# A fourth seven-product pair in every pass over w_down, in a float32 transformer block on one core

## The chip, the cores and the metric

The kernel runs on one core of a Trainium2 chip. The metric is the device time of one execution in microseconds (us), as a median of several executions. Engines are named as in the profile: PE multiplies matrices (its weight loads are PEld), DVE and ACT are the vector and the scalar engine, POOL and SP issue DMA transfers here (POOL the ones that convert or accumulate, SP the plain ones).

## What is computed

One layer over 256 tokens of width 2048, all in float32. The first half (attention and convolution) is not touched by the change. The second half is a gated feed-forward network with 5632 hidden columns:

```python
hn = rms_norm(h, norm2_g[l])
a = jnp.einsum('bsd,df->bsf', hn, w_gate[l])
bu = jnp.einsum('bsd,df->bsf', hn, w_up[l])
h = h + jnp.einsum('bsf,fd->bsd', jax.nn.silu(a) * bu, w_down[l])
```

## The kernel before

**Products.** A float32 factor is split into a rounded part (hi) and the remainder (lo). A product of two factors takes three matmuls: hi by hi, lo by hi, hi by lo. Each matmul has 128 rows, a 128x128 stationary block and 512 moving columns.

**Blocks.** The hidden columns come in 11 blocks of 512 (j0 to j10). For each block w_gate and w_up are multiplied side by side, then u = silu(a) * bu is transposed and stored as factors for w_down. w_down is taken after the blocks j0 to j3, after j4 to j7 and after j8 to j10: here these are the groups A, B and C. A group is multiplied in two passes (n = 0 and n = 2) of two column blocks of 512 each, so there are six passes: A0, A2, B0, B2, C0, C2. Results are added to the output in memory by POOL's DMAs; the last pass reads its own column block back (`so_far`) and writes the sum.

**Units.** A pass is a string of units, written out by hand in `ORDER` and `DOWN`. Two neighbouring 128-row slices of w_down make a "two". A unit `g` or `u` multiplies one two with one of the pass's two column blocks: 12 matmuls. A unit `s` (a "pair") multiplies a two with both column blocks by seven products in place of eight (the scheme of Strassen and Winograd): 21 matmuls in place of 24. In an `s` the weight blocks are first combined on DVE (`pair_sums`), rounded on ACT (`round_raw` for the three raw blocks, `round_pair` for the four sums) and split on DVE (`split_pair`). The factors are combined too (`pair_forms`). For a `g` or `u` there is one rounding on ACT (L342) and one subtraction on DVE (L351). Where the letter is upper-case, ACT writes the negative and a DMA of POOL adds the weights to it (L345, L346), so that DVE has nothing to do.

**Buffers.** Raw weights of pairs have two buffers (`wb`), the sums one (`wt`), the rounded and the split weights of pairs two each (`wh`, `wl`). So a pair's raw rounding writes into the buffer that PE has to be done with two pairs earlier. The eight sums of products lie in eight PSUM banks, four called `acc` and four called `aux`. The aux banks are those of Q2, Q4, Q3 and QX, in the order in which a pass takes them; the bank of QX is taken only by the first `u`, and until then the transposed factors (`ps_a`) go through it. A new pass takes the old pass's banks: those of Q6, Q7, Q5, Q2 and Q4 come free as `bank_sums` (L1196 to L1201) reads them, and Q3's with the first of the two last additions (L1215 in `block_done`, L1249 in `down_done`). Q3 is the last of a pair's seven products (`PRODUCTS`).

**Order.** All instructions are issued in an order that is worked out when the program is built, and each engine runs its own in that order. Before unit t is multiplied, `run_chunks` issues in this order: the splits of units up to t+3, the raw rounding of pairs up to t+5, the weight sums of pairs up to t+5, the rounding of DMA units up to t+5, the rounding of all units up to t+4, and loads up to t+9. While a unit is multiplied, `resume()` lets the waiting pieces of work go one step on: four steps in a pair, two in a `g` or `u`. After a block the piece `block_done` adds and multiplies, waits five steps (`TO_TRANSPOSE`), transposes the first two of the block, and so on. A two that is kept as it is (`transposed`, L957 and L959) is ready three steps after its transposes; a two that serves a pair is ready six steps after them (`pair_forms`: steps 0, 2, 4 and 6). The second two's transposes come two steps after the first is ready. If a unit of w_down is reached before its factors are ready, `multiply_two` or `multiply_pair` issues steps until they are (`while not c["ready"](c): resume()`).

In the last block (j10) the factors of a two that is kept as it is are first copied to a buffer `ac` (L955), which for the second two has the tag `sum2`, the one that `pair_forms` uses for its sums `fs`.

Of the kernel before, what the change touches and what calls it, by code (L numbers as in the profile page):

```python
# [13 lines left out]
F32 = mybir.dt.float32  # L14
F32R = mybir.dt.float32r
AF = mybir.ActivationFunctionType
ALU = mybir.AluOpType
AX = mybir.AxisListType

P = 128  # L20
D = 2048
S = 256
NM = S // P
# [8 lines left out]
KD = D // P  # L32
N = 512
# [52 lines left out]

Q1, Q6, Q7, Q5, Q2, Q4, Q3, QX = range(8)

PRODUCTS = ((Q6, 5, 1), (Q7, 6, 2), (Q5, 4, 3), (Q1, 0, 5), (Q2, 1, 6), (Q4, 2, 0), (Q3, 3, 4))

DOWN = (dict(pairs=((1, 0), (1, 1), (2, 0)), order=("sgGsgGgsuUuUu",) * 2),
        dict(pairs=((4, 0), (4, 1), (5, 0)), order=("sgGsgGgsuUuUu",) * 2),
        dict(pairs=((8, 0), (8, 1), (9, 0)), order=("sGsGgsUUu", "sGsGGsUUu")))

RAW_AHEAD = 5
LOAD_AHEAD, DMA_AHEAD, SUMS_AHEAD, HI_AHEAD, LO_AHEAD = 9, 5, 5, 4, 3


BLOCKS = 2 * KD + 1

TO_TRANSPOSE = 5

# [12 lines left out]
def tile_block(  # L115
# [4 lines left out]
    nc = tc.nc  # L120
    PSUM = bass.MemoryType.PSUM
    act, dve, pool, pe, sp = nc.scalar, nc.vector, nc.gpsimd, nc.tensor, nc.sync
# [17 lines left out]
    make_identity(nc, ident)  # L140
    arena = [const.tile([P, BLOCKS, P], F32R, tag=f"l{x}", name=f"l{x}") for x in ("hi", "lo")]
    neghalf = once.tile([P, 8], F32, tag="neghalf", name="neghalf")
# [26 lines left out]
    def col(key, k):  # L169
        return cols[:, AT[key] + k : AT[key] + k + 1]  # L170
# [80 lines left out]
    def start(gen):  # L251
        running.append(gen)
# [13 lines left out]
    def room(n, hold=0):  # L266
        while held[0] + n > AUX:
            yield
        held[0] += hold
# [574 lines left out]
    def out_done(n, ps):  # L844
        cs = slice(n * N, (n + 1) * N)
        for m in range(NM):
            dve.tensor_tensor(h[m][:, cs], h[m][:, cs], ps[m], ALU.add)
        for m in range(NM):
            pool.dma_start(out=out[m * P : (m + 1) * P, cs], in_=h[m][:, cs])
        if n == 2:  # L850
            held[0] -= NM
        yield
        for t in range(0, N // P, 2):
            k = n * (N // P) + t
            yield from room(1)
# [12 lines left out]
            for i in range(2):  # L868
                hT[k + i] = (hi[:, i, :], lo[:, i, :])
            yield  # L870
        for m in range(NM):
            square_sum(h[m][:, cs], ss2[m][:, n : n + 1])
        if n == D // N - 1:
            yield
            for m in range(NM):
                ss = small.tile([P, 1], F32, tag="ssh", name="ssh")
                dve.tensor_reduce(ss, ss2[m], AX.X, ALU.add)
                rsqrt_mean(rstd2[m], ss, D, EPS)
            yield
            yield  # L880
            prestack.close()
            ffn["pool"] = fp = ctx.enter_context(tc.tile_pool(name="ffn", bufs=1))
            spare_lhs.extend(fp.tile([P, 2, 2, S], F32R, tag=f"a{x}", name=f"a{x}") for x in ("hi", "lo"))
            start(make_forms())


    ffn = {}
# [39 lines left out]
    def place(g):  # L927

        pairs = DOWN[g]["pairs"]
        at = 7 * len(pairs)  # L930
        fhi, flo = (a[:, :at].rearrange("p (f q) c -> p f q c", f=7) for a in arena)
        twos = [(j, t) for j in range(sum(FGROUPS[:g]), sum(FGROUPS[: g + 1])) for t in range(2) if (j, t) not in pairs]
        free = [arena_two(i) for i in range(at, BLOCKS - 3, 4)]
        free += [tuple(a[:, i] for a in spare_lhs) for i in range(2)]
        assert len(free) >= len(twos)
        down[g] = dict(forms=(fhi, flo), pairs=pairs, twos=twos, at=dict(zip(twos, free)), ready=set())

    down = {}
    spare_lhs = []
# [117 lines left out]
    def pair_sums(c):  # L1057

        b = c["b"]
        c["t"] = t = ffn["pool"].tile([P, 4, N], F32, tag="wt", name="wt")  # L1060
        dve.tensor_tensor(t[:, 2:4], b[:, 1:3], b[:, 0:1].to_broadcast([P, 2, N]), ALU.subtract)  # L1061
        dve.tensor_tensor(t[:, 1], b[:, 1], t[:, 3], ALU.add)
        dve.tensor_tensor(t[:, 0], t[:, 1], b[:, 3], ALU.subtract)  # L1063

    def round_raw(c):
        if "hi" not in c:
            c["hi"] = ffn["pool"].tile([P, 7, N], F32R, tag="wh", name="wh", bufs=2)
            act.copy(c["hi"][:, 4:], c["b"][:, 1:])  # L1068

    def round_pair(c):  # L1070
        round_raw(c)
        act.copy(c["hi"][:, :4], c["t"])  # L1072

    def split_pair(c):
        c["lo"] = ffn["pool"].tile([P, 7, N], F32R, tag="wl", name="wl", bufs=2)
        dve.tensor_tensor(c["lo"][:, 4:], c["b"][:, 1:], c["hi"][:, 4:].bitcast(F32), ALU.subtract)  # L1076
        dve.tensor_tensor(c["lo"][:, :4], c["t"], c["hi"][:, :4].bitcast(F32), ALU.subtract)  # L1077

    def sum_bank(c, i):
        sums = c["sums"]  # L1080
# [5 lines left out]
    def multiply_pair(c):  # L1086
        while not c["ready"](c):
            resume()
        (fhi, flo), p = c["forms"](), c["p"]
        products = PRODUCTS[3:4] + PRODUCTS[:3] + PRODUCTS[4:] if c["done"] else PRODUCTS  # L1090
        for n, (q, f, w) in enumerate(products):
# [51 lines left out]
    def fast_block(order, side_u, side_g, pairs, twos, **kw):  # L1143
# [3 lines left out]
        for unit in order:  # L1147
# [26 lines left out]
    def down_block(g, n):  # L1174

        last = g == len(FGROUPS) - 1 and n == D // N - 2
        ks = lambda jt: (jt[0] * (N // P) + 2 * jt[1], jt[0] * (N // P) + 2 * jt[1] + 1)
        pairs = DOWN[g]["pairs"]
        twos = [(j, t) for j in range(sum(FGROUPS[:g]), sum(FGROUPS[: g + 1])) for t in range(2) if (j, t) not in pairs]
        units = fast_block(DOWN[g]["order"][n // 2], ("w_down", n * N), ("w_down", (n + 1) * N),  # L1180
                           [(q, ks(jt)) for q, jt in enumerate(pairs)], [(jt, ks(jt)) for jt in twos],
# [9 lines left out]
    def bank_sums(q):  # L1191

        fp = ffn["pool"]
        w1 = halfway.pop("w1")
        u2, u3, w4 = (fp.tile([P, N], F32, tag=f"sum{i}", name=f"sum{i}") for i in range(1, 4))
        dve.tensor_tensor(u2, q[Q6], w1, ALU.add)  # L1196
        dve.tensor_tensor(u3, q[Q7], u2, ALU.add)
        dve.tensor_tensor(w4, q[Q5], u3, ALU.add)
        dve.tensor_tensor(u2, q[Q5], u2, ALU.add)  # L1199
        dve.tensor_tensor(w1, q[Q2], w1, ALU.add)  # L1200
        dve.tensor_tensor(u3, q[Q4], u3, ALU.add)  # L1201
        halfway.update(g=(w1, u3), u=(u2, w4))
# [21 lines left out]
    def down_products(n, q, last):  # L1224
        so_far = None
        if last:
            so_far = ffn["pool"].tile([P, 4, N], F32, tag="wt", name="so_far")[:, :NM]
            pool.dma_start(out=so_far, in_=out[:, n * N : (n + 1) * N].rearrange("(m p) n -> p m n", p=P))
        bank_sums(q)
        for m in range(NM):  # L1230
            add_to_out(m, n + 1, halfway["g"][m])
        yield
        if last:
            for m in range(NM):
                dve.tensor_tensor(halfway["u"][m], halfway["u"][m], so_far[:, m], ALU.add)
        halfway["added"] = True
# [104 lines left out]
```

## Time and profile before

| | us |
|---|---|
| median of three runs | 1040.02 (1039.77 to 1040.20) |
| the profiled execution | 1041.07 |
| its span, first to last instruction | 1039.2 |
| PE busy in the span | 1030.1 |
| DVE busy | 862.3 |
| ACT busy | 685.6 |

The profiled execution is 1.05 us above the median of the runs, and 1.87 us of it lie outside the span. PE's busy time is not PE at its peak, since matmuls overlap: one of 512 columns shows 389 ns in the profile, and the next starts 227 ns after it.

The second half as PE runs it, from the start of each block's first product to the start of the next block's (us from the span's start):

| block | from | to | us | matmuls of 512 columns |
|---|---|---|---|---|
| A0 | 513.03 | 555.47 | 42.44 | 183 |
| A2 | 555.47 | 596.95 | 41.48 | 183 |
| B0 | 763.05 | 805.50 | 42.45 | 183 |
| B2 | 805.50 | 846.98 | 41.48 | 183 |
| j10 | 929.54 | 971.31 | 41.77 | 180 |
| C0 | 971.31 | 1004.12 | 32.81 | 135 |
| C2 | 1004.12 | 1034.72 | 30.60 | 135 |

Times of C2 end where a further matmul would have started. A0, B0, j10 and C0 contain transposes besides.

### The profile page before, as it was taken

The numbers are of one execution on the slowest core, as the hardware profiler recorded it, in microseconds if no ns is written. First come the engines' busy times: TensorE is split into PE (matmuls) and PEld (weight loads), VectorE is DVE, ScalarE is ACT, GpSimd is POOL, SyncE is SP. The second block draws the span as 40 slices with busy tenths as digits, with TensorE's granted clock in tenths as the row PEclk, the third lists the DMA queues.
The fourth block names the chain that finished last, engine by engine and source line by source line (L and its number), as shares of the span: only waits on it lengthen the run. The fifth ranks groups of instructions, "written<-read, shape, count | busy, mean of one in ns | idle before, by whom it ended". The sixth has DMA issues, their size and how long they took to land.

```text
span 1039.2 us, 13042 instructions
## 1 busy us (share of the span) xinstructions
PE 1030.1 (99%) x4641; PEld 850.3 (82%) x4641; DVE 862.3 (83%) x1086; ACT 685.6 (66%) x864; POOL 155.4 (15%) x198
## 2 busy tenths in 40 slices
PE   8999999999999999999999999999999999999998
PEld 6888888888888888788888888888888888888886
DVE  5599989898546699999978789999896697998983
ACT  5855568766856567777556567776765666767761
POOL 0040133411100101001002120010001121101021
PEclk9999999999999999999999999999999999999999
DMA  9867766676566669898889998987969999879896
GB/s 357 302 202 211 238 206 213 187 211 176 163 201 231 230 215 281 241 323 240 257 246 298 257 306 267 309 229 249 307 187 285 300 271 331 235 243 298 250 249 129
DMA packets 65777, 258.05 MB, mean 248 GB/s; under 512 B 7344, under 2 KB 8624, under 8 KB 58288
## 3 DMA queue, kind: packets, MB, share of 16 engines
q1 hardware_dynamic: 48656, 201.34, 53.5%
q0 software_dynamic: 16768, 55.58, 28.2%
q8 instruction: 36, 0.59, 0.2%
q10 hardware_dynamic: 288, 0.29, 0.1%
q14 instruction: 29, 0.24, 0.1%
HBM read 248.80 MB, written 8.39 MB: 247 GB/s over the span
## 4 chain that ended last, share of the span: by engine, by line
PE 95%; DVE 2%; ACT 1%; issue 1%; DMA 1%; POOL 0%; SPq 0%; DVEq 0%
PE q L1116 11%; PE q L1120 11%; PE q L1115 11%; PE acc L387 11%; PE acc L382 11%; PE acc L381 11%; PE q L1094 9%; PE q L1096 8%; PE q L1095 8%; PE ps_a L922 1%; DMA raw<-in_wts_dram 1%; PE ps_s L731 1%; PE ps_o L809 0%; DVE y L596 0%; PE ps_h L859 0%
## 5 line engine op out<-in xcount | busy, mean ns | idle before, releaser
L342 ACT CAST whi<-raw 128x1024 fp32r<-128x1024 f32 (+1 forms) x261 | 270.3, 1046 | 105.1 <-PE acc L382 42.0
L351 DVE TENSOR_TENSOR wlo<-raw,whi 128x1024 fp32r<-128x1024 f32 (+1 forms) x173 | 209.0, 1218 | 72.9 <-ACT whi L342 71.4
L381 PE MATMUL acc<-whi,lhi 128*128 128x512 f32 x416 | 164.7, 396 | 1.5 <-ACT lhi L243 1.4
L382 PE MATMUL acc<-whi,llo 128*128 128x512 f32 x416 | 162.8, 391 | 0.7 <-DVE llo L244 0.7
L1077 DVE TENSOR_TENSOR wl<-wt,wh 128x2048 fp32r<-128x2048 f32 x58 | 132.7, 2287 | 20.6 <-ACT wh L1072 20.6
L1068 ACT CAST wh<-wb 128x1536 fp32r<-128x1536 f32 x58 | 86.0, 1483 | 87.5 <-PE q L1095 49.1
L346 POOL DMA_DIRECT2D wlo<-in_wts_dram x74 | 65.0, 889 | 510.4 <-ACT wlo L345 483.6
L1115 PE MATMUL q<-whi,chi 128*128 128x512 f32 x320 | 124.7, 390 | 0.0
L1116 PE MATMUL q<-whi,clo 128*128 128x512 f32 x320 | 124.6, 389 | 0.0
L1072 ACT CAST wh<-wt 128x2048 fp32r<-128x2048 f32 x58 | 110.4, 1904 | 18.5 <-DVE wt L1063 18.4
L1094 PE MATMUL q<-wh,fhi 128*128 128x512 f32 x280 | 109.2, 390 | 0.4 <-DVE sum L1199 0.4
L1096 PE MATMUL q<-wl,fhi 128*128 128x512 f32 x280 | 109.0, 389 | 0.0
L1095 PE MATMUL q<-wh,flo 128*128 128x512 f32 x280 | 109.0, 389 | 0.0
L596 DVE SCALAR_TENSOR_TENSOR y<-upad,cw,y 128x256 f32<-128x256 f32 x240 | 100.8, 488 | 5.3 <-ACT y L589 5.3
L1076 DVE TENSOR_TENSOR wl<-wb,wh 128x1536 fp32r<-128x1536 f32 x58 | 101.6, 1752 | 2.3 <-ACT wh L1068 2.3
L387 PE MATMUL acc<-wlo,lhi 128*128 128x512 f32 x368 | 101.4, 397 | 0.2 <-DVE wlo L351 0.2
L381 PEld LDWEIGHTS acc<-whi,lhi 128*128 128x128 f32 x416 | 78.5, 189 | 18.5 <-ACT lhi L243 1.8
L382 PEld LDWEIGHTS acc<-whi,llo 128*128 128x128 f32 x416 | 78.5, 189 | 17.3 <-DVE llo L244 1.2
L1120 PE MATMUL q<-wlo,chi 128*128 128x512 f32 x320 | 86.9, 393 | 0.0
L387 PEld LDWEIGHTS acc<-wlo,lhi 128*128 128x128 f32 x368 | 68.9, 189 | 14.6 <-DVE wlo L351 0.6
L345 ACT ACTIVATE wlo<-raw 128x1024 fp32r<-128x1024 f32 x74 | 78.1, 1056 | 0.0
L1061 DVE TENSOR_TENSOR wt<-wb 128x1024 f32<-128x1024 f32 x58 | 70.8, 1221 | 1.8 <-DMA wb<-in_wts_dram 1.3
(224 smaller groups left out, 1732.5 us busy)
## 6 DMA issues: line engine op xcount, KB each, us to landing
raw<-in_wts_dram SPq DMA_DIRECT2D x259, 512.0 KB, 5.6
wb<-in_wts_dram SPq DMA_DIRECT2D x57, 1024.0 KB, 8.1
wlo<-in_wts_dram POOLq DMA_DIRECT2D x74, 512.0 KB, 9.3
lod<-in_wts_dram POOLq DMA_DIRECT2D x14, 512.0 KB, 5.8
out_dram<-sum POOLq DMA_DIRECT2D x22, 256.0 KB, 7.2
h<-in_x_dram SPq DMA_DIRECT2D x4, 512.0 KB, 8.4
out_dram<-h POOLq DMA_DIRECT2D x8, 256.0 KB, 4.7
xt<-in_xt_dram SPq DMA_DIRECT2D x7, 256.0 KB, 6.9
```

The lines of the kernel that those rows point to most:

```text
L342: act.copy(c["hi"], c["raw"])
L351: dve.tensor_tensor(c["lo"], c["raw"], c["hi"].bitcast(F32), ALU.subtract)
L381: pe.matmul(ps[m], xhi[:, ms], hi[:, j, :], start=c["first"] and j == 0, stop=False)
L382: pe.matmul(ps[m], xlo[:, ms], hi[:, j, :], start=False, stop=False)
L387: pe.matmul(ps[m], xhi[:, ms], lo[:, j, :], start=False, stop=c["last"] and j == nk - 1)
L1077: dve.tensor_tensor(c["lo"][:, :4], c["t"], c["hi"][:, :4].bitcast(F32), ALU.subtract)
L1094: pe.matmul(ps, fhi[:, f, p, :], c["hi"][:, w], start=bool(first), stop=False)
L1095: pe.matmul(ps, flo[:, f, p, :], c["hi"][:, w], start=False, stop=False)
L1096: pe.matmul(ps, fhi[:, f, p, :], c["lo"][:, w], start=False, stop=bool(last))
L1115: pe.matmul(ps, plain[i][0][:, ms], hi[:, i, :], start=i == 0 and bool(c["first"].get(qs[m])), stop=False)
L1116: pe.matmul(ps, plain[i][1][:, ms], hi[:, i, :], start=False, stop=False)
L1120: pe.matmul(sum_bank(c, qs[m]), plain[i][0][:, ms], lo[:, i, :], start=False, stop=i == 1 and bool(c["last"].get(qs[m])))
```

## The change

Every pass of w_down gets a fourth pair. Groups A and B then have four pairs and four twos (before: three and five), group C four pairs and two twos (before: three and three). The orders are rewritten; that of A and B becomes nearly the one of the gate and up blocks (`sgGsgGsUUsUu`). The fourth pair of group C is the first two of block j10, and the two in the place of the fourth unit is j10's second.

To find room for the factors, `pair_sums` writes its last result over the raw block that nothing needs any more (`b[:, 0]`), so the tile of sums has three blocks in place of four; the arena of factors has 32 blocks in place of 33; the spare factors have three places in place of two; and the descriptor ring of POOL's DMAs has 1024 bytes in place of 2048. The rounding of the sums becomes two copies, of three blocks and of one. The split takes the three sums first and then the four blocks that lie in the raw tile; before, it took the three raw blocks first and then the four sums.

```diff
-PRODUCTS = ((Q6, 5, 1), (Q7, 6, 2), (Q5, 4, 3), (Q1, 0, 5), (Q2, 1, 6), (Q4, 2, 0), (Q3, 3, 4))
+PRODUCTS = ((Q6, 5, 0), (Q7, 6, 1), (Q5, 4, 2), (Q1, 0, 5), (Q2, 1, 6), (Q4, 2, 3), (Q3, 3, 4))
-DOWN = (dict(pairs=((1, 0), (1, 1), (2, 0)), order=("sgGsgGgsuUuUu",) * 2),
-        dict(pairs=((4, 0), (4, 1), (5, 0)), order=("sgGsgGgsuUuUu",) * 2),
-        dict(pairs=((8, 0), (8, 1), (9, 0)), order=("sGsGgsUUu", "sGsGGsUUu")))
+DOWN = (dict(pairs=((1, 0), (1, 1), (2, 0), (2, 1)), order=("sgGsgGsuUsUu",) * 2),
+        dict(pairs=((4, 0), (4, 1), (5, 0), (5, 1)), order=("sgGsgGsuUsUu",) * 2),
+        dict(pairs=((8, 0), (8, 1), (9, 0), (10, 0)), order=("sGsgssUu",) * 2))
-BLOCKS = 2 * KD + 1
+BLOCKS = 2 * KD
+SPARE = 3
...
-        c["t"] = t = ffn["pool"].tile([P, 4, N], F32, tag="wt", name="wt")
-        dve.tensor_tensor(t[:, 2:4], b[:, 1:3], b[:, 0:1].to_broadcast([P, 2, N]), ALU.subtract)
-        dve.tensor_tensor(t[:, 1], b[:, 1], t[:, 3], ALU.add)
-        dve.tensor_tensor(t[:, 0], t[:, 1], b[:, 3], ALU.subtract)
+        c["t"] = t = ffn["pool"].tile([P, 3, N], F32, tag="wt", name="wt")
+        dve.tensor_tensor(t[:, 1:3], b[:, 1:3], b[:, 0:1].to_broadcast([P, 2, N]), ALU.subtract)
+        dve.tensor_tensor(t[:, 0], b[:, 1], t[:, 2], ALU.add)
+        dve.tensor_tensor(b[:, 0], t[:, 0], b[:, 3], ALU.subtract)
...
-        act.copy(c["hi"][:, :4], c["t"])
+        act.copy(c["hi"][:, :3], c["t"])
+        act.copy(c["hi"][:, 3], c["b"][:, 0])
...
-        dve.tensor_tensor(c["lo"][:, 4:], c["b"][:, 1:], c["hi"][:, 4:].bitcast(F32), ALU.subtract)
-        dve.tensor_tensor(c["lo"][:, :4], c["t"], c["hi"][:, :4].bitcast(F32), ALU.subtract)
+        dve.tensor_tensor(c["lo"][:, :3], c["t"], c["hi"][:, :3].bitcast(F32), ALU.subtract)
+        dve.tensor_tensor(c["lo"][:, 3:], c["b"], c["hi"][:, 3:].bitcast(F32), ALU.subtract)
...
-    nc = _bacc.Bacc("TRN2", target_bir_lowering=False, num_devices=1, dynamic_dma_scratch_size=2048)
+    nc = _bacc.Bacc("TRN2", target_bir_lowering=False, num_devices=1, dynamic_dma_scratch_size=1024)
```

The tiles of the spare factors and of `so_far` follow suit (`[P, SPARE, 2, S]`, `[P, 3, N]`).

More of the change, by code (lines that the diff above doesn't have):

```diff
@@ L882, in out_done @@
             ffn["pool"] = fp = ctx.enter_context(tc.tile_pool(name="ffn", bufs=1))
-            spare_lhs.extend(fp.tile([P, 2, 2, S], F32R, tag=f"a{x}", name=f"a{x}") for x in ("hi", "lo"))
+            spare_lhs.extend(fp.tile([P, SPARE, 2, S], F32R, tag=f"a{x}", name=f"a{x}") for x in ("hi", "lo"))
             start(make_forms())
@@ L933, in place @@
         free = [arena_two(i) for i in range(at, BLOCKS - 3, 4)]
-        free += [tuple(a[:, i] for a in spare_lhs) for i in range(2)]
+        free += [tuple(a[:, i] for a in spare_lhs) for i in range(SPARE)]
         assert len(free) >= len(twos)
@@ L1226, in down_products @@
         if last:
-            so_far = ffn["pool"].tile([P, 4, N], F32, tag="wt", name="so_far")[:, :NM]
+            so_far = ffn["pool"].tile([P, 3, N], F32, tag="wt", name="so_far")[:, :NM]
             pool.dma_start(out=so_far, in_=out[:, n * N : (n + 1) * N].rearrange("(m p) n -> p m n", p=P))
```

## The prediction

> **What bounds the kernel now.** I read the page's busy times and chain first, then the groups by line, then the busy times of each pass, then the order of time on single engines in the last passes.
>
> ```profile
> span 1039.2 us, 13042 instructions
> PE 1030.1 (99%) x4641; PEld 850.3 (82%) x4641; DVE 862.3 (83%) x1086; ACT 685.6 (66%) x864; POOL 155.4 (15%) x198
> PE 95%; DVE 2%; ACT 1%; issue 1%; DMA 1%; POOL 0%; SPq 0%; DVEq 0%
> ```
>
> PE is on the chain for 95% of the span, so a matmul less is time won, as long as the others keep up. What one is worth is read from starts, not from durations (389 ns, overlapping). Two single units in a row, in the chain in order of time:
>
> ```profile
> 590.77 0.91 PE q L1120 x4
> 593.49 0.91 PE q L1120 x4
> ```
>
> 12 matmuls take 593.49 - 590.77 = 2.72 us, 0.2267 each: 2.72 for a single unit, 4.76 for a pair (21). Now the busy times by pass (us, PE, PEld, DVE, ACT, POOL): A0, A2, block j10, C0, C2.
>
> ```profile
> 513.03:555.47 42.44, 42.44 (x192) 35.13 (x191) 33.71 (x34) 26.64 (x25) 5.27 (x6) 1.00 0.79 228
> 555.47:596.95 41.48, 41.48 (x184) 34.35 (x183) 31.32 (x30) 24.41 (x22) 7.04 (x8) 1.00 1.00 278
> 929.54:971.31 41.77, 41.77 (x189) 34.57 (x188) 37.48 (x41) 31.61 (x31) 5.22 (x6) 1.00 0.87 260
> 971.31:1004.12 32.81, 32.24 (x145) 25.97 (x143) 29.35 (x30) 25.10 (x25) 3.63 (x5) 1.00 0.89 264
> 1004.12:1033.81 29.69, 29.69 (x132) 24.59 (x131) 17.29 (x19) 8.74 (x8) 8.64 (x10) 1.00 0.79 142
> ```
>
> In A2 DVE has 10 us to spare. In C0 it has 3.5 us, and C0 alone takes 2.2 us more than its 135 matmuls (30.60). j10 exceeds its 180 matmuls (40.80) by 0.97: two sets of transposes, 0.48 each. C0 has two sets as well, so 1.2 us of it are waits. They are here, on DVE:
>
> ```profile
> 966.79 0.68 DVE L1196 TENSOR_TENSOR sum<-q,sum 128x512 f32<-128x512 f32 x1
> 970.77 1.75 DVE L1076 TENSOR_TENSOR wl<-wb,wh 128x1536 fp32r<-128x1536 f32 x1
> 974.64 1.28 DVE L1215 TENSOR_TENSOR sum<-q,sum 128x512 f32<-128x512 f32 x2
> 977.04 1.22 DVE L1061 TENSOR_TENSOR wt<-wb 128x1024 f32<-128x1024 f32 x1
> 979.63 1.22 DVE L351 TENSOR_TENSOR wlo<-raw,whi 128x1024 fp32r<-128x1024 f32 x1
> 980.76 1.75 DVE L1076 TENSOR_TENSOR wl<-wb,wh 128x1536 fp32r<-128x1536 f32 x1
> 984.63 0.69 DVE L959 TENSOR_TENSOR llo<-ac,lhi 128x512 fp32r<-128x512 f32 x1
> 985.24 1.22 DVE L1061 TENSOR_TENSOR wt<-wb 128x1024 f32<-128x1024 f32 x1
> 987.83 0.69 DVE L959 TENSOR_TENSOR llo<-ac,lhi 128x512 fp32r<-128x512 f32 x1
> ```
>
> The factors of j10 (L959) stand behind a split (980.76) and behind the weight sums of the next pass (985.24), and PE waits for both:
>
> ```profile
> PE q L1116 <- DVE llo L959: 0.6, 2, 0.4
> ```
>
> So DVE keeps issue order, and work for later units delays a factor that PE wants now. The starts give start-to-next times: bank sums 970.77 - 966.79 = 4.0; split 3.9; L1215 with L1217 2.4; weight sums 979.63 - 977.04 = 2.6; a single unit's subtraction 1.1.
>
> **What the change removes.**
>
> ```profile
> L1094 PE MATMUL q<-wh,lhi 128*128 128x512 f32 x126 | 49.3, 391 | 0.0
> ```
>
> 126 is 6 passes x 3 pairs x 7. A fourth pair replaces 24 matmuls by 21 in each: 18 x 0.2267 = 4.1 us less PE work, 0.7 a pass. A2 and B2 should keep it: DVE gains a pair (2.6 + 3.9) and loses two subtractions (2.2), 35.6 of 40.8 us.
>
> **A0 and B0: small loss.**
>
> ```profile
> 528.38 0.68 DVE L959 TENSOR_TENSOR alo<-ps_a,ahi 128x512 fp32r<-128x512 f32 x1
> ```
>
> This factor, j3's last, is now wanted by the sixth unit, 2 pairs, 3 singles and two transposes after 513.03: 531.7, its second matmul at 531.9. On DVE a subtraction (1.1) and the fourth pair's sums (2.6) come ahead of it: ready at 528.38 + 3.7 + 0.7 = 532.8. 0.9 us late, 1.8 for both; between 0 and 3.7 for both if that queue moves by a microsecond.
>
> **C0: where it goes wrong.** New order: pair 1, G, pair 2, g, pair 3, pair 4, U, u. g multiplies j10's second two. Its factors are ready after 5 steps, 6 for the first two (now a pair's) and 2 + 3 more: step 16. When PE comes to g, 4 + 2 + 4 = 10 steps are gone; so six are issued at once, behind everything already issued for pairs 3 and 4 and the next pass. (Before, a single step was forced.) In order, in the clock of the rows above:
>
> DVE: pair 1's split now waits for the rounding of the sums first, 1.1 us later; so bank sums end at 971.9, pair 2's split at 975.8. Then the sums of pair 3 (978.4), which now stand ahead of L1215: its first half ends at 979.1, the rest at 980.8.
>
> ```profile
> 975.39 0.48 PE L1094 MATMUL q<-wh,lhi 128*128 128x512 f32 x1
> ```
>
> This is pair 1's last product, which starts in the bank that L1215 frees; it started as soon as that was done. Now it waits until 979.1: **3.7 us**, pair 1 ends at 979.8.
>
> ACT: rows for a pair's rounding and for what stands behind it, and who holds up the raw rounding:
>
> ```profile
> 979.75 1.91 ACT L1072 CAST wh<-wt 128x2048 fp32r<-128x2048 f32 x1 [0.17 <-DVE wt L1063]
> 981.56 0.58 ACT L955 COPY ac<-ps_a 128x512 f32<-128x512 f32 x1
> ACT wh L1068 <- PE q L1095: 49.1, 20, 4.4
> ```
>
> The copy of the transposed factors (L955, now L969) stands behind the rounding of a pair; now that is pair 4, whose raw rounding (1.4) waits for PE to be done with pair 2. For the first two's forms I take block j2's rows (DVE 1.5, ACT 1.1):
>
> ```profile
> 442.40 0.28 DVE L975 SCALAR_TENSOR_TENSOR fs<-af 128x128 f32<-128x128 f32 x1
> 443.87 1.75 DVE L1076 TENSOR_TENSOR wl<-wb,wh 128x1536 fp32r<-128x1536 f32 x1
> ...
> 437.28 0.57 ACT L969 COPY af<-ps_a 128x512 f32<-128x512 f32 x1
> 438.41 1.04 ACT L342 CAST whi<-raw 128x1024 fp32r<-128x1024 f32 x1
> ```
>
> After a wait PE may also run slow. At the start of the kernel (the third figure from the end of a row is the granted clock):
>
> ```profile
> 8.00:10.00 2.00, 0.64 (x4) 0.20 (x2) 0.52 (x1) 1.60 (x3) 0.00 (x0) 1.00 1.04 390
> 10.00:12.00 2.00, 1.25 (x5) 0.79 (x6) 2.00 (x4) 1.90 (x4) 0.00 (x0) 1.00 1.03 405
> 12.00:14.00 2.00, 2.00 (x7) 1.62 (x6) 1.85 (x4) 1.70 (x4) 0.00 (x0) 0.62 1.00 371
> 14.00:16.00 2.00, 2.00 (x6) 1.52 (x6) 1.62 (x3) 0.65 (x2) 0.00 (x0) 0.53 1.01 375
> ```
>
> PE was busy for 1.9 of 4 us, and then the clock was 0.62 and 0.53 for 4 us: 4 - 2 x (0.62 + 0.53) = 1.7 us lost. I charge 1.6 for each of three waits that leave PE as idle. [...]
>
> So: G with transposes and slow clock ends at 979.8 + 2.7 + 0.5 + 1.6 = 984.6, pair 2 at 989.3. Pair 4: raw rounding 990.9, three sums rounded 992.4. DVE has meanwhile split pair 3 and summed pair 4 (989.3); it splits pair 4 (996.3), makes the first forms (997.8), sums C2's first pair (1000.4), the last form (1001.0), which frees the buffer for ACT's copy (1001.7) and rounding (1002.3), and then subtracts (1003.0). **PE has been ready for g since 989.8.** g ends at 1003.0 + 2.5 + 1.6 = 1007.1, pairs 3 and 4 at 1016.6, U and u at 1022.1. Before: 1004.1. C0 is 18 us longer, its saved 0.7 included.
>
> **C2.** DVE was held too: the split of its pair 1 needs a raw rounding that waits for pair 3 (1011.9): ends 1018.9; sums of pair 2 1021.5, bank sums 1025.5, split 1029.4, sums of pair 3 1032.0, and only then the first last addition of C0 (1032.7), which frees the bank for pair 1's last product. PE, from 1022.1 and 0.9 late through the bank sums, wants it at 1027.1: 5.6 us more. Pair 1 ends at 1033.4, G (1.6 for the clock) 1037.7, pair 2 1042.5, g 1045.2, pair 3 1049.9, pair 4 (split by 1049.5) 1054.7. Before, the last pair ended and the first of three singles began 0.23 after this:
>
> ```profile
> 1026.33 0.39 PE L1096 MATMUL q<-wl,lhi 128*128 128x512 f32 x1
> wb<-in_wts_dram SPq DMA_DIRECT2D x57, 1024.0 KB, 8.1
> out_dram<-sum POOLq DMA_DIRECT2D x22, 256.0 KB, 7.2
> ```
>
> From there to the span's end it is 1039.2 - 1026.6 = 12.6, with two singles 9.9: 1064.6. The last accumulating DMA (bank sums to 1055.6, two issues, 7.2) lands at about the same time and adds nothing. Loads: `wb` buffers come free 2.2 us later, since the split reads them last; 8.1 us on, none of the steps above waits for one.
>
> **Hidden.** The rounding in two copies costs ACT about 0.1 us a pair, off the chain. The ring:
>
> ```profile
> 1003.07 1.81 POOL L1222 DMA_DIRECT2D out_dram<-sum  x2 [9.35 <-DVE sum L1200]
> 1008.14 1.77 POOL L1222 DMA_DIRECT2D out_dram<-sum  x2 [1.46 <-DVE sum L1249]
> ```
>
> With two more issues between them, six went out within the 7.2 us of a landing, at no longer issue times. The old ring held about that, the new one at least half. No row shows a full ring: 0 is my value, one landing (7.2) the upper end.
>
> **Sum.** 1064.6 - 1039.2 = 25.4; less 2.7 (A0 to B2), plus 1.8: 24.5. On 1041.07 that is 1065.6; on the median, 1.05 lower, 1064.5.
>
> **Rivals.**
> *Only the long wait slows the clock.* Two times 1.6 less: 1061.3. For it: the long wait is 13 us, the others 3.7 and 5.6; against it, the four rows at 8 to 16 us.
> *DVE's order alone*, no slow clock, no wait for the raw rounding: from 971.9 to g's factor DVE has 25.8 us of work (pair 2's split, sums and splits of pairs 3 and 4, the next pass's sums: 19.5; L1215 with L1217, one subtraction, the forms and two last factors: 6.3), so g has it at 997.7 and C0 ends 11 us late instead of 18; the same steps onward end at 1055.8, the median at 1055.7.
> *DVE's total only.* If PE met no single late factor: DVE's work from 971.9 to the last split (six pairs 39, pair 2's split 3.9, bank sums 4, the rest 10.8: 57.7) ends at 1029.6, and PE wants it at 1022.3 (971.3 + 30.9 + 29.9, less the last pair and two singles, plus 0.4): 7.3 - 4.1 later, 1043. The waits for L959 speak against.
> *Not slower.* If the six steps come out ahead of pair 4's split and C2's sums, g's factor needs no more than step 16's own ACT and DVE times, and PE runs on: 1036. It decides at 984.4, where PE wants the factor; DVE would need 12.5 us of work by then, not 25.8. Against it speaks the order of the rows at 984.63 to 987.83.
> *The ring fills.* POOL waits for a landing at C0's end: 1072.
> *The matmuls don't go*: PE's count would stay at 4641.
>
> **Chances.** Forecast: 0.43. Only the long wait slow: 0.27. DVE's order alone: 0.11. DVE's total: 0.04. Not slower: 0.09, of which 0.02 within 0.2% because a wait eats the gain. Ring: 0.06. The range 1048 to 1069 leaves out the ring and the last two. 0.2% is about what a measurement of this kernel tells from no change. Slower 0.91, same 0.02, faster 0.07.
>
> **What would show it.** C0 at 50 us and C2 at 40; PE's longest wait ahead of the fourth unit of C0, put down to L957 or L959; one of about 4 and one of about 5 us, for L1215 and L1249; a granted clock near 0.5 behind them; A2 and B2 at 40.8. No wait above 2 us in C0, or g's L959 ahead of the split of pair 4, would prove me wrong.

## The result

The changed kernel takes 1069.29 us, the median of five runs (1066.79 to 1072.45), the kernel before 1040.03 beside it. The ratio is 1.0281, with a 95% interval of 1.0267 to 1.0296. The forecast was 1064.5 in a range of 1048 to 1069: the sign and the losses in C0 and C2 were right, but block j2 lost 5.75 us for which the forecast had no term, and the time lies just above the range. The profiled execution took 1072.45, 31.4 more than that of before (1041.07); it is the longest of the five, 3.2 above their median. The places below are compared in these two executions.

The page of the changed kernel: span, busy times, and the shares of its chain.

```profile
span 1070.7 us, 13116 instructions
...
PE 1037.5 (97%) x4623; PEld 854.0 (80%) x4623; DVE 894.9 (84%) x1127; ACT 695.7 (65%) x931; POOL 150.2 (14%) x193
...
PE 84%; DVE 9%; issue 3%; ACT 2%; DMA 1%; POOL 0%; SPq 0%; DVEq 0%; ACTq 0%
```

PE runs 4623 matmuls in place of 4641: the 18 are gone, as announced. But PE's share of the chain falls from 95% to 84%, and DVE's rises from 2% to 9%. PE's waits in the second half (what PE waited for: us in total, times, the longest):

```profile
PE q L1118 <- ACT ahi L959: 8.2, 1, 8.2
PE q L1097 <- DVE sum L1252: 5.9, 1, 5.9
PE ps_a L924 <- ACT af L971: 3.8, 1, 3.8
PE q L1097 <- DVE sum L1218: 3.5, 1, 3.5
PE q L1097 <- DVE sum L1199: 3.3, 1, 3.3
PE q L1119 <- DVE alo L961: 0.6, 1, 0.6
```

Line numbers are 2 or 3 higher than before: L1218 and L1252 were L1215 and L1249, L1199 was L1196, L959 and L961 were L957 and L959. The waits of 8.2 and 3.8 are the long one of the forecast, split by j10's second transposes; those for L1218 and L1252 are the two for a bank. The wait for L1199 was not in the forecast. It stands at the start of block j2, far ahead of any pass over w_down. The busy times by block show it too (from:to, length, busy us of PE, PEld, DVE, ACT and POOL with counts, granted clock, DMA share, GB/s). First the changed kernel, blocks j2, A0, A2, C0 and C2, then j2 of the kernel before:

```profile
428.73:477.04 48.31, 44.97 (x189) 36.58 (x188) 46.02 (x57) 32.32 (x38) 4.34 (x5) 0.93 0.90 271
518.81:561.52 42.71, 42.06 (x189) 34.49 (x188) 38.47 (x38) 31.60 (x34) 3.82 (x5) 1.00 0.81 253
561.52:602.32 40.80, 40.80 (x181) 33.78 (x180) 35.46 (x33) 25.60 (x26) 7.10 (x9) 1.00 0.99 284
975.64:1027.84 52.20, 36.74 (x141) 28.79 (x140) 34.56 (x38) 23.40 (x27) 1.77 (x2) 0.80 0.42 135
1027.84:1065.64 37.80, 31.90 (x130) 25.64 (x129) 28.72 (x30) 11.77 (x13) 7.03 (x8) 0.91 0.56 128
```

```profile
428.70:471.26 42.56, 42.14 (x190) 34.42 (x188) 41.80 (x52) 30.41 (x32) 4.29 (x5) 1.00 0.90 270
```

A2 loses its 0.7 us at a granted clock of 1.00. C0 is 19.4 us longer and C2 8.1 (29.69 before, to the same matmul). j2 is 5.75 longer, although the change gives it no matmul more or less, and its granted clock is 0.93.

The blocks of all profiled executions, from first product to first product (us; C2 to a matmul of its last unit, as in the prediction's row of 29.69):

| | j2 | A0 | A2 | B0 | B2 | C0 | C2 |
|---|---|---|---|---|---|---|---|
| before | 42.56 | 42.44 | 41.48 | 42.45 | 41.48 | 32.81 | 29.69 |
| changed | 48.31 | 42.71 | 40.80 | 42.08 | 40.80 | 52.20 | 37.80 |
| raw blocks' part first | 43.48 | 42.24 | 40.80 | 42.25 | 40.80 | 50.18 | 37.64 |
| split in three | 42.80 | 42.04 | 40.80 | 41.84 | 40.80 | 47.13 | 35.60 |
| split's halves exchanged | 48.87 | 45.98 | 40.80 | 43.40 | 40.80 | 51.64 | 37.78 |
| group C undone | 47.62 | 42.72 | 40.80 | 42.07 | 40.80 | 34.13 | 30.59 |
| C undone, raw blocks' part first | 43.52 | 42.25 | 40.80 | 42.24 | 40.80 | 33.18 | 29.84 |
| C undone, split in three | 42.65 | 42.60 | 40.80 | 41.83 | 40.80 | 32.45 | 29.69 |
| the same, A0 and B0 reordered | 42.64 | 41.77 | 40.80 | 41.77 | 40.80 | 32.50 | 29.69 |
| fourth pair held | 48.09 | 42.70 | 40.80 | 42.08 | 40.80 | 42.86 | 37.36 |
| fourth pair held, split in three | 42.64 | 41.82 | 40.80 | 41.83 | 40.80 | 39.26 | 35.59 |
| the same, last additions first | 42.69 | 41.82 | 40.80 | 41.84 | 40.80 | 40.08 | 31.56 |

### The profile page after: what moved, and what is told of

Read it like the earlier page. It is cut to its first block, busy times and chain, and to the rows that moved or that the text cites. A ratio compares the mean times of both kernels' runs of the same rounds, so it can differ in the third digit from the quotient of the medians.

```text
span 1070.7 us, 13116 instructions
## 1 busy us (share of the span) xinstructions
PE 1037.5 (97%) x4623; PEld 854.0 (80%) x4623; DVE 894.9 (84%) x1127; ACT 695.7 (65%) x931; POOL 150.2 (14%) x193
## 4 chain that ended last, share of the span: by engine, by line
PE 84%; DVE 9%; issue 3%; ACT 2%; DMA 1%; POOL 0%; SPq 0%; DVEq 0%; ACTq 0%
PE acc L389 10%; PE acc L384 10%; PE acc L383 10%; PE q L1119 9%; PE q L1118 9%; PE q L1123 9%; PE q L1097 8%; PE q L1098 8%; PE q L1099 8%; DVE wl L1080 2%; DMA raw<-in_wts_dram 1%; DVE wt L1063 1%; ACT wh L1074 1%; DVE wl L1079 1%; DVE wt L1064 1%
## 5 line engine op out<-in xcount | busy, mean ns | idle before, releaser
L344 ACT CAST whi<-raw 128x1024 fp32r<-128x1024 f32 (+1 forms) x249 | 257.3, 1044 | 67.5 <-PE acc L384 43.3
L353 DVE TENSOR_TENSOR wlo<-raw,whi 128x1024 fp32r<-128x1024 f32 (+1 forms) x166 | 200.0, 1215 | 33.4 <-ACT whi L344 32.6
L1070 ACT CAST wh<-wb 128x1536 fp32r<-128x1536 f32 x64 | 94.9, 1483 | 148.1 <-PE q L1098 82.0
L1079 DVE TENSOR_TENSOR wl<-wt,wh 128x1536 fp32r<-128x1536 f32 x64 | 112.3, 1755 | 68.5 <-ACT wh L1074 68.4
L1080 DVE TENSOR_TENSOR wl<-wb,wh 128x2048 fp32r<-128x2048 f32 x64 | 146.2, 2285 | 0.0
L348 POOL DMA_DIRECT2D wlo<-in_wts_dram x69 | 60.4, 875 | 548.9 <-ACT wlo L347 508.0
L1074 ACT CAST wh<-wt 128x1536 fp32r<-128x1536 f32 x64 | 94.2, 1472 | 18.0 <-DVE wt L1064 17.9
L1063 DVE TENSOR_TENSOR wt<-wb 128x1024 f32<-128x1024 f32 x64 | 78.0, 1219 | 2.8 <-DMA wb<-in_wts_dram 2.8
L1097 PE MATMUL q<-wh,lhi 128*128 128x512 f32 x168 | 66.5, 396 | 9.4 <-DVE sum L1252 5.9
```

What stands on the lines that cost most here:

```text
L344: act.copy(c["hi"], c["raw"])
L353: dve.tensor_tensor(c["lo"], c["raw"], c["hi"].bitcast(F32), ALU.subtract)
L1080: dve.tensor_tensor(c["lo"][:, 3:], c["b"], c["hi"][:, 3:].bitcast(F32), ALU.subtract)
L1097: pe.matmul(ps, fhi[:, f, p, :], c["hi"][:, w], start=bool(first), stop=False)
```

## The experiments: what block j2 lost

Two things in the new `split_pair` can reach j2, since it serves every pair of the kernel. Its first instruction now reads rounded sums, so it starts behind their rounding (before, it read only the raw blocks' rounding). And its last instruction reads the raw tile, so the next load into it goes out later (17.06 us after the start of j1 in place of 13.75), with the loads that stand behind it in SP's queue. DVE's order of time in block j1, before the change and after (start, duration, what it is; in brackets the idle time ahead of it and what ended that):

```profile
411.94 0.69 DVE L1063 TENSOR_TENSOR wt<-wt,wb 128x512 f32<-128x512 f32 x1
412.55 1.76 DVE L1076 TENSOR_TENSOR wl<-wb,wh 128x1536 fp32r<-128x1536 f32 x1
414.62 2.29 DVE L1077 TENSOR_TENSOR wl<-wt,wh 128x2048 fp32r<-128x2048 f32 x1 [0.31 <-ACT wh L1072]
```

```profile
405.97 0.69 DVE L1065 TENSOR_TENSOR wb<-wt,wb 128x512 f32<-128x512 f32 x1
407.49 1.76 DVE L1079 TENSOR_TENSOR wl<-wt,wh 128x1536 fp32r<-128x1536 f32 x1 [0.82 <-ACT wh L1074]
...
413.34 0.69 DVE L1065 TENSOR_TENSOR wb<-wt,wb 128x512 f32<-128x512 f32 x1
417.20 1.76 DVE L1079 TENSOR_TENSOR wl<-wt,wh 128x1536 fp32r<-128x1536 f32 x1 [3.17 <-ACT wh L1074]
```

Before, the raw part of the split ran while ACT rounded the sums, and DVE lost 0.31 in this pair. After, the first of these splits waits 0.82, and the next one 3.17, because ACT came late to the rounding. The last three splits that run in j1 wait 4.81 in all (0.82, 3.17, 0.82), against 1.08 before; the difference, 3.73, is what the first bank sum behind them comes later (the table at the end of this section). The reason is in ACT's order of time in the changed kernel:

```profile
412.41 1.05 ACT L344 CAST whi<-raw 128x1024 fp32r<-128x1024 f32 x1 [4.44 <-DMA raw<-in_wts_dram]
413.37 1.06 ACT L347 ACTIVATE wlo<-raw 128x1024 fp32r<-128x1024 f32 x1
414.33 1.47 ACT L1070 CAST wh<-wb 128x1536 fp32r<-128x1536 f32 x1
415.69 1.47 ACT L1074 CAST wh<-wt 128x1536 fp32r<-128x1536 f32 x1
```

The rounding stands behind a wait of 4.44 for a weight load. So both readings were open: the late start, or the late release of the raw tile.

**Raw blocks' part first.** The tile comes free early again, and the split starts behind one short rounding (0.6 us) in place of the long one.

```diff
-        act.copy(c["hi"][:, :3], c["t"])
         act.copy(c["hi"][:, 3], c["b"][:, 0])
+        act.copy(c["hi"][:, :3], c["t"])
...
-        dve.tensor_tensor(c["lo"][:, :3], c["t"], ...)
         dve.tensor_tensor(c["lo"][:, 3:], c["b"], ...)
+        dve.tensor_tensor(c["lo"][:, :3], c["t"], ...)
```

> The changed kernel, with the split taking the four blocks of the raw tile first and the three sums last, so that the raw tile comes free after the first of the two instructions, as before the change. Theory 1 (block j2 lost 5.75 us because the raw tile is freed last, so the load into it, the loads behind it in SP's queue and the roundings that need them are late) and theory 2 (j2 lost it because the split has to wait for the rounding of all three sums before its first instruction) both expect j2 back at 42.6 us and no wait of PE above 1 us there: 1063.5 us in all. C0 and C2 stay near 52 and 38, since their waits come from the order of issue. Rival 3 (j2's wait comes from the extra copy on ACT or from the ring): j2 stays near 48.

Measured: 1064.65 (ratio to before 1.0232, interval 1.0218 to 1.0246), j2 at 43.48, PE's waits there 0.6 and 0.4. Most of j2's loss is gone, 0.9 stays. Both theories expected j2 back at 42.6, so this run doesn't tell them apart.

**Split in three.** The raw blocks first, which need no rounded sum; the tile is still freed last.

```diff
+        dve.tensor_tensor(c["lo"][:, 4:], c["b"][:, 1:], ...)
         dve.tensor_tensor(c["lo"][:, :3], c["t"], ...)
-        dve.tensor_tensor(c["lo"][:, 3:], c["b"], ...)
+        dve.tensor_tensor(c["lo"][:, 3], c["b"][:, 0], ...)
```

> The changed kernel, with the split in three instructions: the three raw blocks first (which need no rounded sum, as before the change), then the three sums, then the sum that lies in the raw tile. The raw tile is still freed last. Theory 1 (release of the raw tile): j2 keeps its wait ahead of the bank sums (3 us) and stays at 47 to 49 us; about 1069. Theory 2 (late start of the split): the wait goes, j2 at 42.6; about 1063.5.

Measured: 1057.81 in one run, j2 at 42.80. The late release is there, and j2 has lost only 0.2. Four more kernels below have this split and the same code up to j2, and there j2 takes 42.64 to 42.69; the changed split stands in two more, with 47.62 and 48.09. For the whole, the better of the two forecasts was 1063.5; 5.7 more are gone, because C0 (47.13) and C2 (35.60) gain too: 5.1 and 2.2 us of their loss go with the split's late start.

**The split's two halves exchanged**, the rounding left alone: the release comes early, the start even later, behind both roundings.

```diff
-        dve.tensor_tensor(c["lo"][:, :3], c["t"], ...)
         dve.tensor_tensor(c["lo"][:, 3:], c["b"], ...)
+        dve.tensor_tensor(c["lo"][:, :3], c["t"], ...)
```

> The changed kernel with the two instructions of the split exchanged, the rounding left in its order: the split starts even later (it needs the last of the two roundings), but the raw tile comes free with its first instruction. Theory (the late start and the late release of the raw tile make j2's loss together, through the loads in SP's queue; each alone costs below 1 us): j2 loses more than with the raw blocks' rounding first (43.5), since each of four splits starts another 0.5 late, but less than in the changed kernel (48.3): 44 to 46, and no wait of ACT above 2.5 us for a raw tile. Rival (the late start alone makes it): j2 at 48 or more. C0 and C2 as in the changed kernel or 1 us longer; 1065 to 1069.

Measured: 1076.35 in one run, j2 at 48.87. My theory, that late start and late release do it together, missed: I expected 44 to 46 us. The rival held. A0 and B0 lose too, 45.98 and 43.40 in place of 42.71 and 42.08. DVE in j1 of this run:

```profile
405.94 0.69 DVE L1065 TENSOR_TENSOR wb<-wt,wb 128x512 f32<-128x512 f32 x1
407.97 2.29 DVE L1079 TENSOR_TENSOR wl<-wb,wh 128x2048 fp32r<-128x2048 f32 x1 [1.34 <-ACT wh L1075]
```

1.34 where the changed kernel waits 0.82. With the split in three, DVE and ACT at the same place:

```profile
410.53 0.69 DVE L1065 TENSOR_TENSOR wb<-wt,wb 128x512 f32<-128x512 f32 x1
413.26 1.76 DVE L1079 TENSOR_TENSOR wl<-wb,wh 128x1536 fp32r<-128x1536 f32 x1 [2.04 <-ACT wh L1070]
414.94 1.75 DVE L1080 TENSOR_TENSOR wl<-wt,wh 128x1536 fp32r<-128x1536 f32 x1
```

```profile
409.85 1.05 ACT L344 CAST whi<-raw 128x1024 fp32r<-128x1024 f32 x1 [3.82 <-DMA raw<-in_wts_dram]
```

ACT waits 3.82 for the load here too, but DVE needs only the rounding of the raw blocks (L1070) to go on, and the sums are rounded by the time it comes to them.

Two times tell the readings apart, both counted from the start of j1: when the load into the raw tile goes out that SP issues around 400 to 404, and when the first bank sum starts (L1196, L1199 or L1200), for which PE waits in j2:

| | load of the raw tile | first bank sum |
|---|---|---|
| before | 13.75 | 41.41 |
| split in three (start early, release late) | 15.54 | 41.70 |
| raw blocks' part first (start behind the short rounding, release early) | 14.67 | 42.39 |
| changed (start behind the long rounding, release late) | 17.06 | 45.13 |
| halves exchanged (start behind both, release early) | 16.28 | 46.34 |

The loads are not in the order of the sums: with the split in three the load is later than with the raw blocks' part first, and less is lost; with the halves exchanged it is earlier than in the changed kernel, and more is lost. So the late release by itself costs 0.3 us at most. What counts is whether DVE has something to do while ACT rounds the sums. In j1, with one buffer of sums, the sums, their rounding, the split and the next sums are one loop, and each pair adds what DVE waits in it.

## The experiments: what C0 and C2 lost

**Group C undone**: three pairs and the old orders there, all else as changed.

```diff
-        dict(pairs=((8, 0), (8, 1), (9, 0), (10, 0)), order=("sGsgssUu",) * 2))
+        dict(pairs=((8, 0), (8, 1), (9, 0)), order=("sGsGgsUUu", "sGsGGsUUu")))
```

> The changed kernel with group C alone as before the change (three pairs, old orders); groups A and B keep four pairs. If C0 and C2 lose their time to the order in which the fourth pair's work and j10's second factor come, they go back to 32.8 and 29.7 us and the whole is 1040.0 + 5.75 (j2) + 0.3 (A0) - 0.4 (B0) - 1.4 (A2, B2) = 1044.3 us. Rival (the new layout of the sums or the smaller ring costs C0 and C2 something too): C0 and C2 stay more than 1 us above the kernel before, over 1046.

Measured: 1045.41 (1.0046, interval 1.0031 to 1.0062). C0 falls from 52.2 to 34.1 and C2 from 37.8 to 30.6. Without the fourth pair and its order nearly all of the loss there is gone; 1.3 and 0.9 us stay, so the rival is right in part: the new layout of the sums costs C0 and C2 something too.

**Group C undone, raw blocks' part first.** Both edits from above.

> Both edits: group C as before the change, and the raw tile's blocks split first. If the two causes are separate and add up, j2 is back at 42.6 and A and B keep what their fourth pair saves: 1040.0 + 0.3 - 0.4 - 1.4 = 1038.5 us, 0.15% faster than before the change. If the rest of the change costs something that I haven't found: 1040 or more.

Measured: 1039.66 (0.9994, interval 0.9986 to 1.0003), 1.1 above the expectation and not told from the kernel before. By the table 0.96 stay in j2 and 0.4 and 0.15 in C0 and C2; A0 is 0.5 shorter than expected and B0 0.2 longer.

**Fourth pair held.** The direct test of the mechanism: nothing is taken away. C0's fourth pair's roundings and split, and the weight sums of C2's first pair, are only issued behind the six steps that make j10's second factor.

```diff
+                held = lambda i: t < chunks[i].get("not_before", 0)
-                until("part", part_of, t + 1 + LO_AHEAD)
+                until("part", part_of, t + 1 + LO_AHEAD, may=lambda i: not held(i))
...
+        if g == 2 and n == 0:
+            s["not_before"] = len(chunks) - len(units) + 4
+        elif g == 2:
+            units[0]["sums_not_before"] = len(chunks) - 2 * len(units) + 4
```

(`raw`, `round` and `sums` are held in the same way; `s` is the last pair of the pass.)

> The changed kernel with one thing moved: the raw rounding, the rounding and the split of C0's fourth pair, and the weight sums of C2's first pair, are issued behind the six steps that make j10's second factor, and no longer ahead of them. The amount of work of each engine stays. Theory (order): the factor is ready some 9 us earlier, at 998 in the clock of the changed kernel, PE's longest wait falls from 12 (8.2 and 3.8) to about 3, C0 from 52 to 43 us, C2 stays at 35 to 38 with its wait of 5 for the bank: 1057 to 1061 us. Rival (DVE and ACT have too much to do in C0 and C2, whatever the order): what the factor gains the fourth pair or C2 loses again, above 1065.

Measured: 1060.75 (1.0188, interval 1.0172 to 1.0203), C0 at 42.86, C2 at 37.36. Order of time on DVE, first of the changed kernel, then of this one:

```profile
997.51 1.76 DVE L1079 TENSOR_TENSOR wl<-wt,wh 128x1536 fp32r<-128x1536 f32 x1 [3.38 <-ACT wh L1074]
...
1002.86 1.22 DVE L1063 TENSOR_TENSOR wt<-wb 128x1024 f32<-128x1024 f32 x1
...
1005.44 0.69 DVE L986 TENSOR_TENSOR llo<-fs,lhi 128x512 fp32r<-128x512 f32 x1
1007.49 0.69 DVE L961 TENSOR_TENSOR alo<-ac,ahi 128x512 fp32r<-128x512 f32 x1 [1.36 <-ACT ahi L959]
```

```profile
995.12 0.28 DVE L979 SCALAR_TENSOR_TENSOR fs<-af 128x128 f32<-128x128 f32 x1
...
996.81 0.69 DVE L988 TENSOR_TENSOR llo<-fs,lhi 128x512 fp32r<-128x512 f32 x1
998.86 0.69 DVE L963 TENSOR_TENSOR alo<-ac,ahi 128x512 fp32r<-128x512 f32 x1 [1.35 <-ACT ahi L961]
1001.61 1.76 DVE L1081 TENSOR_TENSOR wl<-wt,wh 128x1536 fp32r<-128x1536 f32 x1 [2.06 <-ACT wh L1076]
```

In the changed kernel the split of pair 4 (997.51) and the sums of C2 (1002.86) stand ahead of the factor, whose last part starts at 1007.49 (L961); in the other it starts at 998.86 (L963), and the split comes behind it, early enough. The same work in another order makes C0 9.3 us shorter, and nothing comes back in C2. DVE's total is not the bound.

**Fourth pair held, split in three.** Both edits from above.

> The order of the run before this one, with the split in three instructions (raw blocks first). If what both edits save is separate: the 1057.8 us of the three-part split alone less some 9: 1047 to 1050, with j2 at 42.8. If both edits save the same wait in C0: 1054 or more.

Measured: 1049.83 in one run, C0 39.26, C2 35.59. PE's waits in group C:

```profile
PE q L1100 <- DVE sum L1259: 4.8, 1, 4.8
PE q L1121 <- ACT ahi L961: 2.1, 1, 2.1
PE q L1100 <- DVE sum L1225: 2.0, 1, 2.0
```

The gain of holding the pair is 8.0 here, 8.5 without the split in three. As far as single runs tell, the two edits are nearly separate.

**The same, last additions first.** The two waits for a bank were put down to the third pair's sums, which stand ahead of the last additions. Here these sums come behind them.

```diff
+        if g == 2:
+            units[4]["sums_not_before"] = len(chunks) - len(units)
```

> The run before it (fourth pair held, split in three) with the weight sums of the third pair of C0 and of C2 issued behind the last additions that free the bank for the first pair's last product, and no longer ahead of them. Theory: both waits for these additions get 2.6 us shorter, 2.0 to below 0.3 in C0 and 4.8 to 2.2 in C2. C0 doesn't gain by it, since its next wait, for j10's second factor, is set by DVE's order and grows from 2.1 by what PE is early (to 4 or 5): C0 39 us. C2 gains the 2.6 and what the slow clock takes behind its wait: 32 to 33 us; 1046 to 1047 in all. Rival (these waits are set by something else on DVE): C2 stays at 35.6.

Measured: 1046.62 in one run, C0 40.08, C2 31.56. PE's waits in group C:

```profile
PE q L1121 <- ACT ahi L961: 5.8, 1, 5.8
PE q L1100 <- DVE sum L1261: 2.2, 1, 2.2
```

The wait of 2.0 in C0 is gone and that in C2 fell from 4.8 to 2.2, as expected. C0 gains nothing, because PE comes earlier to the factor and waits 5.8 in place of 2.1; it is even 0.8 longer, where 39 was expected.

**The ring alone**, in the kernel before.

```diff
-    nc = _bacc.Bacc("TRN2", target_bir_lowering=False, num_devices=1, dynamic_dma_scratch_size=2048)
+    nc = _bacc.Bacc("TRN2", target_bir_lowering=False, num_devices=1, dynamic_dma_scratch_size=1024)
```

> The kernel before with the ring of 1024 bytes alone. If the smaller ring costs nothing, as I predicted: within 0.1% of the kernel before (1040). Rival (the ring fills where POOL issues many transfers in a row): PE waits behind POOL's transfers appear in C0 or C2, up to 7 us more.

Measured: 1040.13, ratio 0.9999 (0.9990 to 1.0008). The ring costs nothing here, and in the changed kernel no wait of PE in the second half is put down to POOL.

## The experiments: a version that beats both

**Group C undone, split in three.**

> Group C as before the change, groups A and B with four pairs, and the split in three instructions, the raw blocks first (they need no rounded sum). From the blocks of the runs so far: j2 42.8 (+0.24), A0 and B0 42.0 and 41.8 (-0.4 and -0.6), A2 and B2 40.8 (-0.7 each), C0 and C2 32.8 and 29.7 as before: 1040.0 - 2.1 = 1037.9 us, faster than before the change by 0.2%. If the start of the split behind the rounding of the sums isn't what C0 and C2 still lose in the kernel with the raw blocks first and group C undone (0.5 us together): 1038.4.

Measured: 1037.80, ratio 0.9971 (0.9960 to 0.9982): 0.3% faster than the kernel before, as worked out from the table. C0 and C2 are back at 32.45 and 29.69, so what they kept losing with group C undone was the start of the split.

**The same, A0 and B0 reordered**: the fourth pair's sums in A0 and B0 wait for one unit, so that j3's and j7's last factor goes ahead of them.

```diff
+        if g < 2 and n == 0:
+            s["not_before"] = len(chunks) - len(units) + 5
```

> The version with group C undone and the split in three, with the weight sums of the fourth pair of A0 and B0 held back for one unit, so that j3's and j7's last factor stands ahead of them on DVE. If that order is what PE waits for in A0 (0.5) and B0 (0.2): A0 falls from 42.6 to 41.8 us, B0 stays at 41.8; 1037.0 to 1037.8 us.

Measured: 1037.08, ratio 0.9967 (0.9954 to 0.9979). A0 falls from 42.60 to 41.77 and B0 from 41.83 to 41.77, as expected. But three more executions with the same code up to there (split in three, sums not held) have A0 at 42.04, 41.82 and 41.82, so most of A0's 0.83 may be chance. The intervals of the two versions overlap, and which is faster is not shown. Both beat the kernel before and the changed one.

## Why the prediction came out as it did

**The 18 matmuls, A2 and B2:** right. 40.80 in both, 0.68 less each.

**A0 and B0:** 0.9 late each was forecast for the last factor. A0's unit with it takes 3.66 in place of 2.72, 0.94 late; B0's only 0.31. A0's number was luck. Counted from the start of the pass, PE wants the factor at 18.9 us; it was done at 16.0 before the change, and the sums ahead of it bring it to 18.8, as B0 shows with the split in three (41.83, so 0.06 lost). The subtraction that the forecast added besides stood ahead of the factor already (L351 at 523.38, between the factors at 522.77 and 528.38). In the changed kernel the late split adds 0.24 in both, and in A0 another 0.62, by which the factor before it is late already (done at 11.11 in place of 10.49); where DVE loses that is not shown. With the sums held back the factor is done at 16.2, and both passes take 41.77. Together the groups A and B gained 1.5 where 0.9 was forecast.

**C0:** the mechanism and the place were right, waits for waits. The bank: 3.7 forecast, 3.5 measured. The factor's subtraction was forecast to end at 1003.0; it ends at 1008.2 (the row at 1007.49), and C0 began 4.3 later, so the chain of DVE and ACT took 0.9 more than forecast. It starts with pair 4's raw rounding, which waits for PE to be done with pair 2, and PE was 1.0 late there, because the slow clock took 2.6 in place of 1.6. PE's two waits add up to 12.0 (8.2 and 3.8), not 13.2: the forecast counted to the end of the subtraction, and PE starts on the rounded part, at 1007.51. C0 is longer by 19.4, with 18 forecast.

**C2:** 5.6 forecast for the bank, 5.9 measured; C2 with what follows is 7.8 longer in place of 7.4. Putting the last addition ahead of the third pair's sums takes 2.6 us off this wait (4.8 to 2.2 in those two runs); what makes up the rest was not tested.

**The clock:** 1.6 was charged for each of three waits. Each took some 2.5 to 2.6 from PE, an estimate: at a granted clock of 0.50, half of the time from PE's restart to the end of the slow stretch (the stretches are listed at the end). For the first, PE restarts at 983.40 (the row ahead of it is the restart in j2):

```profile
432.91 0.80 PE L1097 MATMUL q<-wh,fhi 128*128 128x512 f32 x1 [3.34 <-DVE sum L1199]
...
983.40 0.80 PE L1097 MATMUL q<-wh,lhi 128*128 128x512 f32 x1 [3.52 <-DVE sum L1218]
```

The stretch ends at 988.68, and (988.68 - 983.40) / 2 = 2.64. That PE runs slow behind each of the three was right, the size not. The rival that only the long wait slows the clock falls: the granted clock was 0.50 behind the waits of 3.5 and 5.9 as well.

**j2, where the prediction failed:** the sum has no term for any block ahead of A0. The step that failed is the price of the split's later start. It was seen, but charged once, in C0: "pair 1's split now waits for the rounding of the sums first, 1.1 us later". It holds for every pair of the kernel, and everywhere else it was put at nothing; of the rounding only the second copy was priced, "about 0.1 us a pair, off the chain". The second copy is not what cost the time: it stays in the run with the split in three, where j2 is back at 42.80. In j1 sums, rounding and split are one loop, so there it *is* the chain, and the kernel before already had a wait at the bank sums of j1, so no margin (PE's waits of the kernel before):

```profile
PE q L1094 <- DVE sum L1199: 0.4, 1, 0.4
```

The runs show 3.3 us of wait and 3.1 of slow clock, (439.13 - 432.91) / 2, in its place, less the 0.8 that j2 lost before already (42.56, where j10 takes 41.77): 5.6 of the 5.75. The step beside it, that the later release of `wb` is waited for by "none of the steps above", looked only at group C; in j2 the release by itself cost 0.3 us at most.

The sum over the profiled executions: forecast 24.5, plus 5.75 in j2, 1.4 in C0, 0.4 in C2 and behind, less 0.6 in A and B, gives 31.45; measured 31.4. These terms are the blocks' own differences, so the sum shows only that nothing else changed. On the medians the change costs 29.3, and the forecast is 4.8 too low.

**Rivals:** DVE's order alone (1055.7) left out the clock and the waits of ACT. DVE's total falls with the fourth pair held, where the same work takes less time. Nothing shows a full ring. PE runs 4623 matmuls, so the 18 are gone.

## What to carry over

An edit in a helper is priced at every place that calls it, and first at the place with the least margin; the question there is what the engine has to do while the input that now comes last is made. Where an order is issued ahead by unit counts, look for work of later units that stands in front of a factor which is wanted now: here a reorder alone made one pass 9.3 us shorter. A fourth pair paid (0.7 us a pass) in groups A and B, where its factors are early; in C none of the orders tried made it pay.

## What the runs showed of the hardware

**PE ran at half the clock behind the waits.** In the second half of the changed kernel the granted clock was 0.50 in four stretches and 1.00 outside them:

| from | to | us | PE's waits there |
|---|---|---|---|
| 432.30 | 439.13 | 6.8 | 3.3, to 432.91 |
| 981.85 | 988.68 | 6.8 | 3.5, to 983.40 |
| 998.92 | 1012.57 | 13.7 | 3.8, to 998.53; 8.2, to 1007.51 |
| 1036.46 | 1043.29 | 6.8 | 5.9, to 1038.15 |

The first two in rows of 2 us (columns as above, the clock is the third from the end):

```profile
428.00:430.00 2.00, 1.57 (x7) 0.95 (x6) 2.00 (x3) 1.77 (x2) 0.24 (x1) 1.00 0.57 59
430.00:432.00 2.00, 0.00 (x0) 0.00 (x0) 1.93 (x3) 0.44 (x1) 0.00 (x0) 1.00 1.01 199
432.00:434.00 2.00, 1.09 (x3) 0.90 (x4) 1.79 (x4) 1.55 (x2) 0.00 (x0) 0.58 1.04 430
434.00:436.00 2.00, 2.00 (x6) 1.58 (x5) 2.00 (x4) 0.32 (x1) 0.00 (x0) 0.50 0.97 393
436.00:438.00 2.00, 2.00 (x6) 1.54 (x5) 2.00 (x5) 2.00 (x4) 0.00 (x0) 0.50 0.57 234
438.00:440.00 2.00, 2.00 (x7) 1.56 (x7) 2.00 (x3) 1.74 (x2) 0.79 (x1) 0.72 0.00 0
978.00:980.00 2.00, 1.88 (x9) 1.22 (x7) 2.00 (x1) 0.00 (x0) 0.00 (x0) 1.00 0.00 0
980.00:982.00 2.00, 0.00 (x0) 0.00 (x0) 1.97 (x3) 0.00 (x0) 0.00 (x0) 0.96 0.28 53
982.00:984.00 2.00, 0.60 (x2) 0.51 (x3) 1.97 (x5) 0.00 (x0) 0.00 (x0) 0.50 0.98 410
984.00:986.00 2.00, 2.00 (x6) 1.61 (x5) 2.00 (x3) 1.30 (x1) 0.00 (x0) 0.50 0.96 391
986.00:988.00 2.00, 2.00 (x6) 1.52 (x6) 0.70 (x2) 2.00 (x4) 0.00 (x0) 0.50 0.48 195
988.00:990.00 2.00, 2.00 (x11) 1.62 (x10) 2.00 (x2) 1.98 (x3) 0.00 (x0) 0.83 0.00 0
```

In the two rows ahead of the first stretch PE was busy for 1.57 of 4 us, ahead of the second for 1.88. Slow clock behind a wait was what I expected, but not its length: each of these waits has 6.8 us of 0.50, where I had charged for 4 us at 0.62 and 0.53. What sets the length is not shown.

**The same wait cost 1.7 us in one run and nothing in another.** A wait of 2.0 us in C0, in the run with the split in three and in the one with the fourth pair held besides:

```profile
971.00:973.00 2.00, 1.51 (x7) 0.93 (x5) 1.97 (x3) 0.00 (x0) 0.00 (x0) 1.00 0.46 90
973.00:975.00 2.00, 0.50 (x2) 0.46 (x3) 1.97 (x5) 0.00 (x0) 0.00 (x0) 1.00 0.89 377
975.00:977.00 2.00, 2.00 (x10) 1.62 (x10) 2.00 (x4) 1.70 (x2) 0.00 (x0) 1.00 0.99 401
977.00:979.00 2.00, 2.00 (x13) 1.65 (x12) 2.00 (x3) 2.00 (x3) 0.00 (x0) 1.00 0.44 180
```

```profile
971.00:973.00 2.00, 1.35 (x6) 0.77 (x5) 1.93 (x4) 0.00 (x0) 0.00 (x0) 1.00 0.43 66
973.00:975.00 2.00, 0.66 (x3) 0.57 (x4) 2.00 (x4) 0.00 (x0) 0.00 (x0) 1.00 1.02 430
975.00:977.00 2.00, 2.00 (x7) 1.57 (x6) 2.00 (x3) 1.84 (x2) 0.00 (x0) 0.56 0.98 401
977.00:979.00 2.00, 2.00 (x9) 1.51 (x8) 2.00 (x3) 2.00 (x3) 0.00 (x0) 0.59 0.37 152
```

In both PE was busy for 2.01 of the first 4 us. In the first the granted clock stayed at 1.00 in the next 4 us, in the second it was 0.56 and 0.59 there: 4 - 2 x (0.56 + 0.59) = 1.7 us lost, an estimate. What decides between the two is not shown. The runs of the changed kernel spread over 5.7 us and those of before over 0.4. The spread goes with the clock: from the longest of the five runs to the shortest, the mean granted clock is 0.982, 0.984, 0.987, 0.989 and 0.989. Why it differs from run to run is not shown, since only one execution of each was profiled.
